# Layer 0 mixer of a two-layer diffusion backbone: projection and attention issued among the S5 batches, rotation tables on VectorE, attention normalised at its outputs

## The chip, the cores and the metric

One core of one Trainium2 chip runs the whole program. The metric is device time of one launch in microseconds (us). Engines: PE is TensorE, DVE is VectorE, ACT is ScalarE, POOL is GpSimd, SP issues the DMAs.

## The reference

Two layers are applied to 128 context tokens and 512 latent tokens (640 columns). The change touches the mixer of layer 0 only, which runs two head groups beside each other on one input projection:

```python
def _even_mixer_latent(h, ck, cv, x0_re, x0_im, w_in, w_out, s5p, rpb):
    u, q, k, v = _even_split(h, w_in)                 # u: 512 columns, q k v: 8 heads of 64
    a_out, _, _ = _s5_mixer(u, x0_re, x0_im, *s5p)
    b_out = _neighbourhood_attention(q, k, v, ck, cv, rpb)
    return concatenate([a_out, b_out], -1) @ w_out
# S5: x_t = lam_bar * x_(t-1) + b_bar u_t (complex, 32 groups, 64 states), forward and backward,
#     y = Re(c x) summed over both directions + d u; z = gelu(y); out = z * sigmoid(z @ w_glu + b_glu)
# attention: p = softmax([q k_window + bias, q ck]); out = p_loc v_window + p_ctx cv
```

The context tokens go through the same mixer with a zero start state and plain softmax attention. The rest (modulation, squared-ReLU MLP, the DeltaNet of layer 1, norms) is the same before and after.

## The kernel before

Every large matmul splits its f32 weights into a high and a low part (`weight`: ACT writes `whi`, L194; `wlo` is a subtraction, L196) and issues three matmuls per 128x128 weight tile (L205 to L207), 320 columns each. `self.lov = 3` around the projection puts two of three `wlo` subtractions on DVE, the others on POOL.

**S5.** The 32 groups go through in four batches of 8 (`s5_batch`), each with two directions d (`s5_unit`). A unit builds input taps `bp` (L785 to L787) and output taps `ct` (L798 to L800) on DVE, transposes `bp` (L792), computes `W` from the inputs `U` (L809), and turns the complex recurrence into a real one: `rotate` multiplies by a table `rt` of cosines and sines (L832, L833, after a swap of the halves by two DMAs, L825 and L826) and adds (L834), one real scan runs (L844 or L846), and a second `rotate` turns back. For d = 0 the adds L787 and L834 run on POOL, for d = 1 on DVE. `s5_taps` makes the taps inside a chunk (L914, L919), `s5_back` the outputs (L947 to L951) and the GELU (L964 to L969).

The table of a batch comes from `s5_tables`: a copy of nine start values (L877), then three doublings from 8 to 64 entries in `turns` (L863 to L868, six POOL operations each), then three DMAs that copy it to the other partitions and to the second direction (L880, L881). `rt` has two buffers, which are the two directions of one batch: the next table starts when the last rotations of the batch before are done with them.

**Attention.** For four head pairs five blocks of 128 queries: scores (L1003) into tags `pa` and `pc`, bias (L1008), maximum (L1010), its negation (L1011), exponential with sum on ACT (L1013), reciprocal (L1015), normalisation of the probabilities on POOL (L1017); three blocks later the transposes (L1023), the products with v (L1031) and the split into high and low part (L1040, L1041). `att` lies where the normed input `hn` of the projection was, so it opens when the projection is done.

**Order.** The program is written down once; a scheduler with a cost model of its own places every instruction on its engine's queue, by data and by priority. Before, the four batches stand first (priority 4000), the projection follows at lower priority and fills in, attention stands after both. Each queue then runs strictly in order.

Of the kernel before, what the change touches and what calls it, by code (L numbers as in the profile page):

```python
# [148 lines left out]
class Build:  # L149
# [465 lines left out]
    def s5_params(self, P, sm, ring):  # L615
# [151 lines left out]
        self.turns(e[:, 0], e[:, 1], 1, 8, wk[:, 2], wk[:, 3], nc.gpsimd)  # L767

    def s5_unit(self, b, d, P, U, tb):
# [17 lines left out]
        (V if d else nc.gpsimd).tensor_tensor(bpv, bpv, t1[:, :, :8], op=AD)  # L787
# [66 lines left out]
    def turns(self, c, s, n0, n1, w1, w2, eng):  # L854

        M, AD, SU = ALU.mult, ALU.add, ALU.subtract
        n = n0
        while n < n1:
            xr, xi = c[:, :, 1:n + 1], s[:, :, 1:n + 1]
            yr = c[:, :, n:n + 1].to_broadcast(list(xr.shape))  # L860
            yi = s[:, :, n:n + 1].to_broadcast(list(xr.shape))
            a1, a2 = w1[:, :, :n], w2[:, :, :n]
            eng.tensor_tensor(a1, xr, yr, op=M)  # L863
            eng.tensor_tensor(a2, xi, yi, op=M)
            eng.tensor_tensor(c[:, :, n + 1:2 * n + 1], a1, a2, op=SU)
            eng.tensor_tensor(a1, xr, yi, op=M)
            eng.tensor_tensor(a2, xi, yr, op=M)
            eng.tensor_tensor(s[:, :, n + 1:2 * n + 1], a1, a2, op=AD)  # L868
            n *= 2

    def s5_tables(self, b, P):

        nc = self.nc
        t = [self.tl([128, 2, 8, 65], "rt") for d in range(2)]
        w1 = self.PA.tile([128, 8, 32], F32, name="rt1")
        w2 = self.PA.tile([128, 8, 32], F32, name="rt2")
        nc.gpsimd.tensor_copy(t[0][:, :, :, 0:9], self.s5e[:, :, 8 * b:8 * b + 8])  # L877
        self.turns(t[0][:, 0], t[0][:, 1], 8, 64, w1, w2, nc.gpsimd)
# [14 lines left out]

    def s5_batch(self, b, P, U):
        ct, S = [None] * 2, [None] * 2
        tb = self.s5_tables(b, P)
        for d in range(2):
            ct[d], S[d] = self.s5_unit(b, d, P, U, tb[d])
        return U, ct, S
# [75 lines left out]
    def attention(self, hp, qkv, ab, P):  # L975
# [16 lines left out]
        def block(qs, keys, vts, kind):  # L992

            n = len(vts) * 128
            sc = []
# [9 lines left out]
            if kind is None:  # L1005
                V.tensor_copy(S[:, :, :n], two(pl, n))
            else:
                V.tensor_tensor(S[:, :, :256], two(pl, 256), biases[kind], op=ALU.add)  # L1008
                nc.scalar.activation(S[:, :, 256:n], two(pc, 128), AF.Copy)
            V.tensor_reduce(ss[:, :, 0:1], S[:, :, :n], axis=AX.X, op=ALU.max)  # L1010
            V.tensor_scalar(ss[:, :, 1:2], ss[:, :, 0:1], -1.0, None, op0=ALU.mult)  # L1011
            for hh in range(2):
                nc.scalar.activation(S[:, hh, :n], S[:, hh, :n], AF.Exp, bias=ss[:, hh, 1:2],  # L1013
                                     accum_out=ss[:, hh, 2:3])
            V.reciprocal(ss[:, :, 3:4], ss[:, :, 2:3])  # L1015
            for hh in range(2):
# [12 lines left out]
            for hh in range(2):  # L1029
                for i, v in enumerate(vts):  # L1030
                    nc.tensor.matmul(po[64 * hh:64 * hh + 64, 0:128], v[:, 64 * hh:64 * hh + 64],  # L1031
                                     pT[hh][:, 128 * i:128 * i + 128], start=(i == 0), stop=(i == len(vts) - 1),
                                     tile_position=(0, 64 * hh))
            if kind is None:
                o, hi, lo = po[:, 0:128], *(t[:, 0:128] for t in ab)
            else:
                o = po[:, 0:128].rearrange("p (c r) -> p c r", r=8)
                c0 = (qs.start - 128) // 8
                hi, lo = (t[:, 128:].rearrange("p (r c) -> p c r", r=8)[:, c0:c0 + 16] for t in ab)
# [31 lines left out]
    def even_s5(self, hn, P, fillers):  # L1071
# [13 lines left out]
        def ev(n, h, p):  # L1085
# [32 lines left out]
        def project():  # L1118
            def fill(m):
                for f in fillers[2 * m:2 * m + 2]:  # L1120
                    self.mod_half(*f, P, tag="pa")
            self.lov = 3
            self.gemm([A["wine"][4 + n] for n in range(12)], hn, ev, after=fill)
            self.lov = 0
        ust = self.ust
        zs = []
        held = None
        Us = [self.s5_load(t) for t in ust[:2]]
        for b in range(5):
            if b and b + 2 - 1 < 4:  # L1130
                Us.append(self.s5_load(ust[b + 2 - 1]))
            with tc.high_priority(offset=4000):
                cur = self.s5_batch(b, P, Us[b]) if b < 4 else None
                if cur:
                    kd = self.s5_taps(b, P, cur[1])
            if held:
                with tc.high_priority(offset=-1000):
                    zs.append(self.s5_back(b - 1, P, *held))
            held = (*cur, self.s5_pull(kd)) if cur else None
# [3 lines left out]
        fo = P.tile([64, 128], F32, name="fo")  # L1143
        V.tensor_copy(fo, fp[:64, :128])
        nc.sync.dma_start(out=self.O["sr"].rearrange("a b d g n -> (a b d g) n"), in_=fo[:, 0:64])
        nc.sync.dma_start(out=self.O["si"].rearrange("a b d g n -> (a b d g) n"), in_=fo[:, 64:128])
        with tc.high_priority(offset=-500):
            project()
        return zs, qkv
# [701 lines left out]
    def run(self, stop=None):  # L1851
        nc, A, tc = self.nc, self.A, self.tc
        with contextlib.ExitStack() as es:
# [35 lines left out]
            with contextlib.ExitStack() as ph:  # L1889
# [11 lines left out]
                with phase("l0") as P:  # L1901
# [5 lines left out]
                    zds, qkv = self.even_s5(hn, P, mods[:0])  # L1907
                    mods = mods[0:]
                    rx.close()
                    with phase("att", "right") as PA:  # L1910
# [17 lines left out]
                    with tc.high_priority(offset=1000):  # L1928
                        ads = self.even_gate(zds, P)
# [66 lines left out]
```

## Time and profile before

| | us |
|---|---|
| median of 3 runs (range) | 2006.68 (2005.63 to 2009.8) |
| profiled execution | 2007.75 |
| its span, first to last instruction | 2005.9 |
| mixer of layer 0, from the last S5 parameters to the gate's end | about 80 to 388 |

PE is busy 90% of the span, DVE 64%, ACT 43%, POOL 45%. The profiled execution lies 1.07 us above the median and 1.85 us above its own span. A busy PE is not PE at its peak: matmuls overlap, and its granted clock varies. The stretch in question is therefore read by itself, with its own waits.

### The profile page before, as it was taken

What the parts mean: (1) busy time and instruction counts of PE and PEld (TensorE: products, weight loads), DVE (VectorE), ACT (ScalarE), POOL (GpSimd) and SP (SyncE); (2) the same over time, 40 slices, a digit from 0 to 9 for tenths busy, and PEclk for the clock granted to TensorE, in tenths of its full rate; (3) what the DMA queues carried; (4) which work ended last, traced back from release to release, by engine and by line L of the source; (5) the groups of instructions that cost most, each with busy time, mean ns of one, the idle gap of its engine ahead of it and who ended that gap; (6) DMA issues with size and microseconds to landing.
All of it is one profiled execution on the core that took longest, in us unless ns stands there. A gap on an engine that the chain in (4) does not pass through costs nothing. (4 is left out here: it accounts for less than half of the span.)

```text
span 2005.9 us, 35754 instructions
## 1 busy us (share of the span) xinstructions
PE 1808.1 (90%) x13476; PEld 1705.7 (85%) x13476; DVE 1285.6 (64%) x2765; ACT 864.1 (43%) x1908; POOL 894.7 (45%) x743
## 2 busy tenths in 40 slices
PE   5778769998999999999888789888998899999998
PEld 3778757897899999998878788787888899999998
DVE  8877866638546372727779998865657936354453
ACT  4333345434326161626554365444324534444362
POOL 2766545362334343454466645532235234334351
PEclk9889889998999999999989899898989899999999
DMA  8334588623422222332586468758844122222221
GB/s 314 111 108 131 133 246 287 237 85 137 158 95 95 73 89 70 113 125 80 154 230 185 124 172 221 210 160 282 284 158 148 63 85 76 83 74 85 84 88 61
DMA packets 206984, 286.60 MB, mean 143 GB/s; under 512 B 54878, under 2 KB 138236, under 8 KB 206812
## 3 DMA queue, kind: packets, MB, share of 16 engines
q1 hardware_dynamic: 206812, 284.33, 44.5%
q8 instruction: 106, 1.74, 0.4%
q14 instruction: 66, 0.54, 0.1%
HBM read 228.87 MB, written 46.82 MB: 137 GB/s over the span
## 5 line engine op out<-in xcount | busy, mean ns | idle before, releaser
L196 POOL TENSOR_TENSOR wlo<-raw,whi 128x1024 fp32r<-128x1024 f32 (+1 forms) x145 | 335.1, 2313 | 393.9 <-ACT whi L194 378.9
L194 ACT ACTIVATE whi<-raw 128x1024 fp32r<-128x1024 f32 (+1 forms) x153 | 153.0, 1000 | 321.1 <-PE pg L206 144.1
L207 PE MATMUL pg<-hidh,wlo 128*128 128x320 f32 (+2 forms) x576 | 178.8, 311 | 0.6 <-POOL wlo L196 0.6
L205 PE MATMUL pg<-hidh,whi 128*128 128x320 f32 (+2 forms) x576 | 179.1, 311 | 0.0
L206 PE MATMUL pg<-hidl,whi 128*128 128x320 f32 (+2 forms) x576 | 179.0, 311 | 0.0
L205 PE MATMUL pg<-h10h,whi 128*128 128x320 f32 x472 | 158.5, 336 | 17.4 <-ACT cb L1312 11.1
L422 DVE SCALAR_TENSOR_TENSOR x<-pg,mod,x 128x128 f32<-128x128 f32 (+2 forms) x132 | 53.8, 436 | 179.5 <-PE pg L207 179.4
L206 PE MATMUL pg<-h10l,whi 128*128 128x320 f32 x472 | 156.4, 331 | 0.0
L207 PE MATMUL pg<-h10h,wlo 128*128 128x320 f32 x472 | 156.1, 331 | 0.0
L205 PE MATMUL pa<-hidh,whi 128*128 128x320 f32 x448 | 138.0, 310 | 2.8 <-ACT whi L194 2.8
L207 PE MATMUL pa<-hidh,wlo 128*128 128x320 f32 x448 | 138.4, 309 | 0.0
L206 PE MATMUL pa<-hidl,whi 128*128 128x320 f32 x448 | 138.2, 309 | 0.0
L422 DVE SCALAR_TENSOR_TENSOR x<-pa,mod,x 128x128 f32<-128x128 f32 (+2 forms) x108 | 43.9, 435 | 137.2 <-PE pa L207 137.2
L507 POOL TENSOR_TENSOR wq<-S,wq 128x512 fp32r<-128x512 f32 x52 | 70.7, 1360 | 115.6 <-ACT wq L506 115.6
L205 PEld LDWEIGHTS pg<-h10h,whi 128*128 128x128 f32 x472 | 95.8, 203 | 19.9 <-ACT cb L1312 11.6
L207 PEld LDWEIGHTS pg<-hidh,wlo 128*128 128x128 f32 x576 | 108.2, 188 | 1.6 <-POOL wlo L196 1.1
L205 PEld LDWEIGHTS pg<-hidh,whi 128*128 128x128 f32 x576 | 108.3, 188 | 0.9 <-issue 0.8
L206 PEld LDWEIGHTS pg<-hidl,whi 128*128 128x128 f32 x576 | 108.2, 188 | 0.4 <-DVE hidl L568 0.3
L1320 DVE SCALAR_TENSOR_TENSOR cv<-cb,cw,cv 128x642 f32<-128x642 f32 x90 | 94.5, 1051 | 7.8 <-ACT cv L1317 6.9
L206 PEld LDWEIGHTS pg<-h10l,whi 128*128 128x128 f32 x472 | 96.3, 204 | 0.6 <-issue 0.4
L207 PEld LDWEIGHTS pg<-h10h,wlo 128*128 128x128 f32 x472 | 95.9, 203 | 0.4
L205 PEld LDWEIGHTS pa<-hidh,whi 128*128 128x128 f32 x448 | 83.9, 188 | 4.4 <-ACT whi L194 3.6
(751 smaller groups left out, 5912.5 us busy)
## 6 DMA issues: line engine op xcount, KB each, us to landing
raw<-in_wff SPq DMA_DIRECT2D x104, 512.0 KB
mraw<-in_wmod SPq DMA_DIRECT2D x96, 512.0 KB
raw<-in_wino SPq DMA_DIRECT2D x33, 512.0 KB
rawx<-in_wff SPq DMA_DIRECT2D x24, 512.0 KB
raw<-in_wine SPq DMA_DIRECT2D x16, 512.0 KB
cka<-pd SPq DMA_DIRECT2D x28, 256.0 KB
ckb<-pd SPq DMA_DIRECT2D x28, 256.0 KB
s5g<-s5g SPq DMA_DIRECT2D x32, 164.0 KB
```

The costliest lines, as they stand in the source:

```text
L194: nc.scalar.activation(hi[:, :kt], raw[:, :kt], AF.Copy)
L196: (nc.vector if self.lov and self.nw % self.lov else nc.gpsimd).tensor_tensor(lo[:, :kt], raw[:, :kt], hi[:, :kt], op=ALU.subtract)
L205: nc.tensor.matmul(p[:, :n], hi[:, k], xh[:, s], start=(k == 0), stop=False)
L206: nc.tensor.matmul(p[:, :n], hi[:, k], xl[:, s], start=False, stop=False)
L207: nc.tensor.matmul(p[:, :n], lo[:, k], xh[:, s], start=False, stop=(k == kt - 1))
L422: nc.vector.scalar_tensor_tensor(x[m][:, s], p[:, ls], g, x[m][:, s], op0=ALU.mult, op1=ALU.add)
L507: (V if j % 2 else nc.gpsimd).tensor_tensor(t[:, 4:8], src, t[:, 0:4], op=SU)
L1320: V.scalar_tensor_tensor(cv, cb[m][:, t:t + 642], cw[:, t:t + 1], cv, op0=M, op1=AD)
```

## The change

Four parts. (1) `turns` works on cosine and sine together: four DVE operations per doubling in place of six on POOL. (2) The adds L787 and L834 of d = 0 go to DVE like those of d = 1. (3) `even_s5` no longer raises and lowers priorities: a generator `s5_steps` yields after each table and each direction. Three steps (batch 0) stand ahead of the projection, one step after every second of its 12 weight tiles (batches 1 and 2), and one after each attention block (batch 3, the last outputs). `self.lov = 3` is gone, so all 12 `wlo` of the projection are on POOL. (4) Attention keeps its exponentials unnormalised; the reciprocal sums are spread over partitions by two matmuls a block against the identity, copied by ACT, and multiplied onto the outputs by DVE. The maximum comes out negated from the reduction, the context block reads its scores in PSUM, and `pT` gets tiles of its own. The copies `ko` and `fo` for the outputs share the three buffers `s5o` of `s5_back`.

```diff
-        self.turns(e[:, 0], e[:, 1], 1, 8, wk[:, 2], wk[:, 3], nc.gpsimd)
+        self.turns(e, 1, 8, wk.rearrange("p a b c -> p (a b c)"))
...
-        (V if d else nc.gpsimd).tensor_tensor(bpv, bpv, t1[:, :, :8], op=AD)
+        V.tensor_tensor(bpv, bpv, t1[:, :, :8], op=AD)
...
-            (V if d else nc.gpsimd).tensor_tensor(out, m, sw, op=op)
+            V.tensor_tensor(out, m, sw, op=op)
...
-            eng.tensor_tensor(a1, xr, yr, op=M)
-            eng.tensor_tensor(a2, xi, yi, op=M)
-            eng.tensor_tensor(c[:, :, n + 1:2 * n + 1], a1, a2, op=SU)
-            eng.tensor_tensor(a1, xr, yi, op=M)
-            eng.tensor_tensor(a2, xi, yr, op=M)
-            eng.tensor_tensor(s[:, :, n + 1:2 * n + 1], a1, a2, op=AD)
+            V.tensor_tensor(a, x, yi, op=M)
+            V.tensor_tensor(y, x, yr, op=M)
+            V.tensor_tensor(y[:, 0], y[:, 0], a[:, 1], op=SU)
+            V.tensor_tensor(y[:, 1], y[:, 1], a[:, 0], op=AD)
...
-                V.tensor_copy(S[:, :, :n], two(pl, n))
+                src = two(pl, n)
...
-            V.tensor_reduce(ss[:, :, 0:1], S[:, :, :n], axis=AX.X, op=ALU.max)
-            V.tensor_scalar(ss[:, :, 1:2], ss[:, :, 0:1], -1.0, None, op0=ALU.mult)
+            V.tensor_reduce(ss[:, :, 1:2], src, axis=AX.X, op=ALU.max, negate=True)
...
-                nc.gpsimd.tensor_scalar(S[:, hh, :n], S[:, hh, :n], ss[:, hh, 3:4], None, op0=ALU.mult)
...
-            pT = [self.tl([128, 384], tag) for tag in ("bp", "bpt")]
+            pT = [P.tile([128, 384], F32, name=f"pT{hh}") for hh in range(2)]
...
+                nc.tensor.matmul(po[64 * hh:64 * hh + 64, 128:256], ss[:, hh, 3:4].to_broadcast([128, 64]), self.ident,
+                                 start=True, stop=True, tile_position=(0, 64 * hh))
+            nc.scalar.activation(rs, po[:, 128:256], AF.Copy)
+            V.tensor_tensor(po[:, 256:384], po[:, 0:128], rs, op=ALU.mult)
...
-                ko = self.tl([128, 128], "ko")
+                ko = self.tl([128, 656], "s5o")[:, 0:128]
...
+        steps = self.s5_steps(P)
+        for _ in range(3):
+            next(steps)
+        def after(m):
+            if m % 2:
+                next(steps)
+        self.gemm([A["wine"][4 + n] for n in range(12)], hn, ev, after=after)
...
                                 open_.append(blk)
+                                next(steps, None)
```

On POOL, at the first table of the S5 batches, before (L877 starts a table, L863 to L868 double it, L787 is the add of `bp`):

```order
L877 COPY rt<-s5e 128x16x9
L940 MEMSET s5o 128x8
L863 TENSOR_TENSOR rt_1080<-rt 128x8x8
L864 TENSOR_TENSOR rt_1081<-rt 128x8x8
L865 TENSOR_TENSOR rt<-rt_1080,rt_1081 128x8x8
L866 TENSOR_TENSOR rt_1080<-rt 128x8x8
L867 TENSOR_TENSOR rt_1081<-rt 128x8x8
L868 TENSOR_TENSOR rt<-rt_1080,rt_1081 128x8x8
L787 TENSOR_TENSOR bp<-bp,s5tmp 128x1024
```

The same place on POOL now (L875 is the copy that starts a table, L196 the low part of a weight):

```order
L1054 MEMSET us 128x8x18 x2
L875 COPY rt<-s5e 128x16x9
L196 TENSOR_TENSOR wlo<-raw,whi 128x1024 x3
L931 MEMSET s5o 128x8
L196 TENSOR_TENSOR wlo<-raw,whi 128x1024
L875 COPY rt<-s5e 128x16x9
L196 TENSOR_TENSOR wlo<-raw,whi 128x1024 x3
```

Between two table starts only weight splits are left. On DVE, where attention begins, before (L832 to L844 are the rotation and scan of batch 3, L1006 the first score copy):

```order
L832 TENSOR_TENSOR s5g<-s5g,rt 128x8x65
L832 TENSOR_TENSOR s5g<-s5g,rt 128x8x17
L833 SCALAR_TENSOR_TENSOR s5g<-s5g,cst,rt 128x8x65
L833 SCALAR_TENSOR_TENSOR s5g<-s5g,cst,rt 128x8x17
L839 MEMSET s5g 128x8
L840 MEMSET s5g 128x8
L844 SCALAR_TENSOR_TENSOR s5g<-s5g 128x656
L1006 COPY sS<-pa 128x2x128
```

On DVE at the same point now (L834 to L867 belong to batch 2 and to the table of batch 3, L1001 is the first maximum):

```order
L834 TENSOR_TENSOR s5s<-s5g 128x656
L864 TENSOR_TENSOR rt_2595<-rt 128x128
L865 TENSOR_TENSOR rt<-rt 128x16x8
L787 TENSOR_TENSOR bp<-bp,s5tmp 128x1024
L851 COPY s5fin<-s5s 128x8
L814 COPY s5g<-s5prm 128x8
L866 TENSOR_TENSOR rt<-rt,rt_2595 128x8x8
L867 TENSOR_TENSOR rt<-rt,rt_2595 128x8x8
L1001 TENSOR_REDUCE ss<-pa 128x2
L799 TENSOR_TENSOR s5tmp<-pwi,s5bc_757 128x1152
```

Attention starts one batch earlier, with the whole of batch 3 still to come on DVE. On PE at the same point, before (L792 and L809 serve batch 3, L1003 are scores):

```order
L792 MATMUL pb<-cst,bp 128x128 x8
L207 MATMUL pg<-h00h_126,wlo 128x320
L1110 MATMUL pc<-cst,qs 128x128
L809 MATMUL pb<-s5s,bpt 128x128 x7
L809 MATMUL pb<-s5s,bpt 128x82
L1110 MATMUL pc<-cst,qs 128x128 x7
L1003 MATMUL pa<-kT,qz_2893 128x128
```

On PE now (L792 and L809 serve batch 2, L993 are scores, L905 the taps of batch 2, L1011 a transpose of probabilities):

```order
L1105 MATMUL pc<-cst,qs 128x128
L792 MATMUL pb<-cst,bp 128x128 x8
L1105 MATMUL pc<-cst,qs 128x128 x7
L809 MATMUL pb<-s5s,bpt 128x128 x7
L809 MATMUL pb<-s5s,bpt 128x82
L993 MATMUL pa<-kT,qz_2569 128x128
L281 MATMUL pa<-mraw,scond 32x256 x4
L993 MATMUL pc<-ckT,qz_2569 128x128 x2
L993 MATMUL pa<-kT,qz_2570 128x128
L993 MATMUL pc<-ckT,qz_2570 128x128 x2
L905 MATMUL pb<-ct,Bb_923 32x128 x16
L1011 MATMUL pg<-cst,sS 128x128
```

The eight transposes and eight input products of a unit stand in both rows; before they are those of the last batch, now those of the last but one.

## Rows read from the trace of the kernel before

**Rows 1.** Stretches: length, then busy us (instructions) of PE, PEld, DVE, ACT, POOL; clock.
```profile
80.50:251.00 170.50, 138.51 (x972) 134.95 (x972) 131.37 (x160) 53.52 (x105) 114.28 (x101) 0.87 0.45 124
251.00:268.75 17.75, 3.18 (x27) 2.71 (x26) 5.16 (x9) 3.19 (x6) 6.46 (x7) 0.71 0.69 183
268.75:376.00 107.25, 105.60 (x873) 81.71 (x873) 77.67 (x198) 62.48 (x181) 55.15 (x51) 0.98 0.83 266
376.00:388.00 12.00, 9.41 (x54) 7.97 (x54) 9.03 (x12) 6.25 (x14) 4.78 (x2) 1.00 0.41 136
```
**Rows 2.** Waits from 80 to 270 us: who waited for whom, total, times, longest.
```profile
ACT s5g L811 <- POOL s5g L834: 32.7, 3, 11.3
DVE s5g L832 <- DMA rt<-rt: 27.8, 4, 11.3
...
PE pb L914 <- ACT s5g L811: 19.9, 3, 7.0
```
**Rows 3.** Timeline of DVE: the first rotation of each batch (start, us, idle before).
```profile
121.43 0.91 DVE L832 TENSOR_TENSOR s5g<-s5g,rt 128x520 f32<-128x520 f32 x2 [11.35 <-DMA rt<-rt]
...
166.73 0.70 DVE L832 TENSOR_TENSOR s5g<-s5g,rt 128x520 f32<-128x520 f32 x1 [6.48 <-DMA rt<-rt]
...
206.36 0.91 DVE L832 TENSOR_TENSOR s5g<-s5g,rt 128x520 f32<-128x520 f32 x2 [0.37 <-DMA rt<-rt]
...
262.52 0.91 DVE L832 TENSOR_TENSOR s5g<-s5g,rt 128x520 f32<-128x520 f32 x2 [9.64 <-DMA rt<-rt]
```
**Rows 4.** DVE from one first rotation to the next, and from the last to 388.
```profile
121.43:166.73 45.30, 37.55 (x46) 0.81 0.37 101
166.73:206.36 39.63, 33.53 (x44) 0.91 0.56 159
206.36:262.52 56.16, 39.05 (x49) 0.84 0.49 135
...
262.52:388.00 125.48, 90.01 (x216) 0.96 0.78 249
```
**Rows 5.** Timeline of POOL: start of two tables, and the end of the second.
```profile
85.42 1.37 POOL L877 COPY rt<-s5e 128x144 f32<-128x144 f32 x1
...
179.53 0.32 POOL L877 COPY rt<-s5e 128x144 f32<-128x144 f32 x1 [5.91 <-issue]
...
197.20 1.73 POOL L868 TENSOR_TENSOR rt<-rt,rt 128x256 f32<-128x256 f32 x1
```
**Rows 6.** Timeline of SP: the first table's DMAs are issued.
```profile
112.00 1.19 SPq L880 DMA_DIRECT2D rt<-rt  x2
```
**Rows 7.** Timeline of DVE: two products of f32 tiles with a broadcast operand.
```profile
80.51 0.29 DVE L743 TENSOR_TENSOR pw<-pwr 128x128 f32<-128x128 f32 x1
...
123.26 1.22 DVE L786 TENSOR_TENSOR s5tmp<-pwi,Bb 128x1024 f32<-128x1024 f32 x1
```
**Rows 8.** DVE groups, shapes apart, 82 to 388 us: count, busy, mean ns.
```profile
L196 DVE TENSOR_TENSOR wlo<-raw,whi 128x1024 fp32r<-128x1024 f32 x7 | 9.5, 1355 | 0.2 <-ACT whi L194 0.2
...
L787 DVE TENSOR_TENSOR bp<-bp,s5tmp 128x1024 f32<-128x1024 f32 x4 | 7.2, 1810 | 0.8 <-DVE s5tmp L786 0.8
...
L1041 DVE TENSOR_TENSOR ab<-pc,ab 128x128 fp32r<-128x128 f32 x20 | 7.2, 362 | 3.6 <-ACT ab L1040 3.3
...
L834 DVE TENSOR_TENSOR s5s<-s5g 128x656 f32<-128x656 f32 x4 | 4.6, 1146 | 0.0
...
L1011 DVE TENSOR_SCALAR ss<-ss 128x2 f32<-128x2 f32 x20 | 3.8, 197 | 0.0
```
**Rows 9.** PE group of attention's products with v, 269 to 376 us.
```profile
L1031 PE MATMUL pc<-bp,vt 128*64 128x128 f32 x72 | 12.1, 287 | 0.0
```
**Rows 10.** Timeline of PE: W of one unit; first and last product of one `s5_back`.
```profile
102.81 1.91 PE L809 MATMUL pb<-s5s,bpt 128*128 128x128 f32 x16
...
276.74 0.49 PE L947 MATMUL pb<-s5s,ct 128*128 128x128 f32 x2
...
283.09 0.39 PE L951 MATMUL pb<-s5s,L 128*128 128x81 f32 x2
```

More of the change, by code (lines that the diff above doesn't have):

```diff
@@ L852, in s5_unit, with turns @@
         return ct, S
-    def turns(self, c, s, n0, n1, w1, w2, eng):
+    def turns(self, t, n0, n1, w):
+        V = self.nc.vector
         M, AD, SU = ALU.mult, ALU.add, ALU.subtract
-        n = n0
+        n, g = n0, t.shape[2]
         while n < n1:
[L859 to L862, printed above, removed]
-            eng.tensor_tensor(a1, xr, yr, op=M)
-            eng.tensor_tensor(a2, xi, yi, op=M)
-            eng.tensor_tensor(c[:, :, n + 1:2 * n + 1], a1, a2, op=SU)
-            eng.tensor_tensor(a1, xr, yi, op=M)
-            eng.tensor_tensor(a2, xi, yr, op=M)
-            eng.tensor_tensor(s[:, :, n + 1:2 * n + 1], a1, a2, op=AD)
+            x, y = t[:, :, :, 1:n + 1], t[:, :, :, n + 1:2 * n + 1]
+            sh = [128, 2, g, n]
+            yr, yi = (t[:, k, :, n:n + 1].unsqueeze(1).to_broadcast(sh) for k in range(2))
+            a = w[:, :2 * g * n].rearrange("p (k g e) -> p k g e", k=2, g=g)
+            V.tensor_tensor(a, x, yi, op=M)
+            V.tensor_tensor(y, x, yr, op=M)
+            V.tensor_tensor(y[:, 0], y[:, 0], a[:, 1], op=SU)
+            V.tensor_tensor(y[:, 1], y[:, 1], a[:, 0], op=AD)
             n *= 2
@@ L892, in s5_load @@
         return U
[L894 to L899, printed above, removed]
     def s5_taps(self, b, P, ct):
@@ L1009, in block @@
                 nc.scalar.activation(S[:, :, 256:n], two(pc, 128), AF.Copy)
[L1010 to L1011 removed]
+                src = S[:, :, :n]
+            V.tensor_reduce(ss[:, :, 1:2], src, axis=AX.X, op=ALU.max, negate=True)
             for hh in range(2):
[L1013 removed]
+                nc.scalar.activation(S[:, hh, :n], src[:, hh], AF.Exp, bias=ss[:, hh, 1:2],
                                      accum_out=ss[:, hh, 2:3])
             V.reciprocal(ss[:, :, 3:4], ss[:, :, 2:3])
[L1016 to L1017 removed]
             yield
[L1019 removed]
+            pT = [P.tile([128, 384], F32, name=f"pT{hh}") for hh in range(2)]
             for hh in range(2):
@@ L1033, in block @@
                                      tile_position=(0, 64 * hh))
+            for hh in range(2):
+                nc.tensor.matmul(po[64 * hh:64 * hh + 64, 128:256], ss[:, hh, 3:4].to_broadcast([128, 64]), self.ident,
+                                 start=True, stop=True, tile_position=(0, 64 * hh))
+            rs = P.tile([128, 128], F32, name="rs")
+            nc.scalar.activation(rs, po[:, 128:256], AF.Copy)
+            V.tensor_tensor(po[:, 256:384], po[:, 0:128], rs, op=ALU.mult)
             if kind is None:
-                o, hi, lo = po[:, 0:128], *(t[:, 0:128] for t in ab)
+                o, hi, lo = po[:, 256:384], *(t[:, 0:128] for t in ab)
             else:
-                o = po[:, 0:128].rearrange("p (c r) -> p c r", r=8)
+                o = po[:, 256:384].rearrange("p (c r) -> p c r", r=8)
                 c0 = (qs.start - 128) // 8
@@ L1117, in ev @@
                 nc.sync.dma_start(out=qkv[hp][m], in_=tmp[n])
[L1118 to L1124, printed above, removed]
+        steps = self.s5_steps(P)
[4 more added lines that the diff above has]
+                next(steps)
@@ L1125, in even_s5, with s5_steps @@
+        self.gemm([A["wine"][4 + n] for n in range(12)], hn, ev, after=after)
+        return steps, qkv
+    def s5_steps(self, P):
+        nc = self.nc
+        self.zs = zs = []
         ust = self.ust
-        zs = []
         held = None
         Us = [self.s5_load(t) for t in ust[:2]]
[L1129 to L1135, printed above, removed]
-            if held:
-                with tc.high_priority(offset=-1000):
-                    zs.append(self.s5_back(b - 1, P, *held))
-            held = (*cur, self.s5_pull(kd)) if cur else None
+        for b in range(4):
+            if 1 <= b < 3:
+                Us.append(self.s5_load(ust[b + 1]))
+            ct, S = [None] * 2, [None] * 2
+            tb = self.s5_tables(b, P)
+            yield
+            ct[0], S[0] = self.s5_unit(b, 0, P, Us[b], tb[0])
+            yield
+            ct[1], S[1] = self.s5_unit(b, 1, P, Us[b], tb[1])
+            kd = self.s5_taps(b, P, ct)
+            if held:
+                zs.append(self.s5_back(b - 1, P, *held))
+            held = Us[b], ct, S, self.s5_pull(kd)
+            yield
+        zs.append(self.s5_back(3, P, *held))
+        yield
@@ L1141, in even_s5 @@
         fp = self.ps("pb")
         nc.tensor.transpose(fp[:64, :128], self.s5fin, self.ident)
-        fo = P.tile([64, 128], F32, name="fo")
-        V.tensor_copy(fo, fp[:64, :128])
+        fo = self.tl([128, 656], "s5o")[0:64, 0:128]
+        nc.vector.tensor_copy(fo, fp[:64, :128])
         nc.sync.dma_start(out=self.O["sr"].rearrange("a b d g n -> (a b d g) n"), in_=fo[:, 0:64])
         nc.sync.dma_start(out=self.O["si"].rearrange("a b d g n -> (a b d g) n"), in_=fo[:, 64:128])
-        with tc.high_priority(offset=-500):
-            project()
```

14 lines of the change are left out of this document (5 added, 9 removed).

## The prediction

> **What bounds the kernel now.** I read the stretches first, then the waits, then each queue's order of time in the stretch that the change touches. From 80.5 to 251 us the projection and S5 run together: PE is busy 138.5 of 170.5 us at a granted clock of 0.87, DVE 131.4, POOL 114.3; then PE has 3.2 us of work in 17.75 us until attention starts; from 268.75 to 376 PE is busy 105.6 of 107.25 us while DVE has 77.7 [rows 1]. So the first stretch is not PE's, the attention stretch is. The reader is to see in the waits who ends what in the first one: DVE waits 27.8 us in all for the table `rt`, ACT 32.7 us for POOL's rotation adds, PE 19.9 us behind that ACT copy [rows 2]. That is one chain: table on POOL, DMA, rotation, add on POOL, buffer free, W copied, PE goes on.
>
> The beat is the batch. First rotations start at 121.4, 166.7, 206.4 and 262.5 us [rows 3], 47.0 us apart on average, with 36.7 us of DVE work in each (37.55, 33.53, 39.05) [rows 4]. A table takes POOL from 179.53 to 198.93, 19.4 us [rows 5] with one rotation add inside, and its copies land later: the first is issued at 112.0 and waited for until 121.4, 9.4 us [rows 3, 6]. After the last first rotation 125.5 us remain to the gate's end at 388, with 90.0 us of DVE work [rows 4].
>
> **The change part by part.**
>
> *Tables on DVE.* Four operations in place of six per doubling, over 16n, 16n, 8n and 8n elements, n = 8, 16, 32: 2688 elements in 12 instructions. No row shows this operation on DVE. The nearest are 0.29 us for 128 elements and 1.22 for 1024 [rows 7]: 0.93/896 = 1.04 ns an element and 0.16 fixed. That gives 2.8 + 1.9 = 4.7 us a table. Bounds: 2.8 (elements alone) and 19.4 (POOL's own time); I take 4.7, as the rows are the same engine and type. The first table starts with POOL's at 85.4 [rows 5], but DVE's order puts both directions' `bp` and `ct` between its pieces; nine more products of 1.2 to 1.6 us and two adds give about 20.5 us, so its DMAs go out at 106 in place of 112.0 [rows 6]. With the same 9.4 us the first rotation comes at 115.5, 6 us earlier.
>
> *Adds on DVE.* Per batch one L787 at 1.8 us and two L834 at 1.0 (the row has 1.146) [rows 8]: 3.8 us. *Weight splits.* Seven of 1.36 us leave DVE in the stretch [rows 8], 2.3 us a batch; POOL has room for all twelve at about 2.4 us, since four tables were most of its 114 us [rows 1, 5]. *Work per batch on DVE:* 36.7 + 4.7 + 3.8 - 2.3 = 42.9 us, 6.2 more than before. Against that stands the idle time: of 47.0 us 10.3 were idle, and the waits for `rt` alone were 6.48, 0.37 and 9.64 [rows 3], 5.5 on average. After its last piece the table now has about 7 us of other DVE work in front of the rotation, which covers most of the 9.4. POOL's adds no longer stand inside the chain. I leave 4 us of waits and take 3 off for DVE operations that POOL slowed; a batch then takes 44 us (40 to 47). So the tables alone buy little per batch: DVE gives up a wait and gets the work instead.
>
> *Batch 3 behind the start of attention.* This is the main term. By the order rows attention's first maximum stands after the first rotations of batch 2, not of batch 3. First rotation of batch 2: 115.5 + 2 x 44 = 203.5. Attention starts 6.2 us after that rotation, as before (268.75 - 262.52) [rows 1, 3]: 210, in place of 268.75. PE can be there: of its 138.5 us, batch 3's unit, one `s5_back` and one set of taps leave (12), so 80.5 + 126.5 = 207. The vacated memory of `hn` and the loads of k and q, which PE waits for, move with it. SP's queue holds the swaps, the tables' copies, `s5_back`'s and the q, k, v loads in program order; a load behind a waiting swap is late, and that is in the 4 us.
>
> *What attention then carries.* On DVE: the 90.0 us of before, plus one whole batch 42.9, two more rotation adds 2.0, 20 products with the spread sums at the price of the nearest PSUM product, 0.362 [rows 8], 7.2; minus 20 negations of 0.197 [rows 8], 3.9, and four score copies of 256 elements, 1.7 estimated from 0.362 for half as many. Sum 136.5; less 3 for POOL's absence 133.5. On PE: unit (two times 1.9 for W [rows 10], the transposes at most as much), one back 276.74 to 283.48 less 1.5 of other work, 5.2 [rows 10], taps 1.1: about 12.5. The 40 spreading matmuls: 80 records at 12.1/72 = 0.168 us [rows 9] would be 13.4; half, if the two halves overlap in their column groups as those of L1031 do: 7. So PE needs 107.25 + 19.5 and the 12 us tail [rows 1], 139 us from 210, to 349. DVE needs 133.5 us of work from 203.5: to 337 without any wait, but both queues run in order and feed each other. Before, DVE idled 28% there because PE was the bound; in the S5 beat without the `rt` waits 12%. I take 14%, near the latter since DVE is now as full: 156 us, so the gate ends at 359.5 in place of 388.
>
> *Normalisation at the outputs.* POOL's multiplications, between exponential and transposes, go; POOL is idle half of that stretch [rows 1], so alone they hold nobody up. What is late next is the output: spread, ACT copy, DVE product, then the two split operations, while the PSUM slot `pc` stays held and PE's next context scores want it. ACT gets 20 copies, some 7 us beside 62.5 of 107 [rows 1]: no bound. `ko` in `s5o` buffers makes an ACT copy wait for `s5_back`'s buffers; at most a few us on an engine with slack, 0 taken.
>
> *Sum.* 359.5 - 388 = -28.5. From 388 to the end the same instructions run, in queues that the scheduler shuffled a little: 0, within 6. From the profiled execution's 2007.75 this gives 1979; the median of the runs lies 1.07 lower, so the sum stands for 1978 to 1979. I predict 1980.
>
> A page's rule would move the beat. The first table took POOL 26.6 us, from 85.4 to 112.0, the third 19.4, each with one add inside [rows 5, 6]: the same operations last differently beside a busy DVE. The Trainium skill, "SBUF — State Buffer", section "SBUF: two separate sides", says that a GpSimd operation and a VectorE operation with two SBUF inputs hold their shared ports exclusively, so that the later one blocks. By it DVE would run at its shortest durations once the tables are gone, about 40 us a batch, which is the quick case below; but the twelve weight splits, now all on POOL, would block DVE in turn, which is why I don't take it whole. The trace of before agrees as far as those two table times go.
>
> **The rivals.**
>
> *Quick case: PE stays attention's bound.* Batches take 40 us (first rotation of batch 2 at 195.5, attention at 202), DVE's work hides beside PE, and the gate ends 139 + 8 us later, at 349. 39 us less: 1969. For it: PE was busy 105.6 of 107.25 us there [rows 1]. Against: DVE's 133.5 us are within 4% of PE's sum.
>
> *Slower: DVE becomes the bound of attention and PE waits in it.* The batch's rotations, scans and taps stand on one queue between the scores' bias and maximum; a wait for a swap then delays the softmax of three open blocks, PE waits for the transposes, and `pc` is held longer. If DVE keeps the 28% idle that it has there now [rows 4], 133.5 us become 186: from 203.5 to 389.5, 2009; with batches of 47 us from 209.5 to 395.5, 2015. It decides from 51 us of waits on. For it: 42.9 + 7.2 us more work on an engine that already took turns with PE. Against: its waits there were PE's, and with less work. The Trainium skill, "Perfetto Trace Analysis", section "Optimizing Scalar/DVE Operations", advises moving work off a saturated VectorE, to GpSimd even, and this change goes the other way; the trace of before has DVE at 77% in S5 and 72% in attention, not yet saturated.
>
> *The change doesn't move attention forward.* The loads of q and k stand behind waiting swaps on SP, and the projection behind waiting S5 matmuls on PE; attention starts only at 235 and carries the batch all the same: 235 + 151 = 386, 2006. Against: PE's 126.5 us of work end well ahead.
>
> **How the numbers follow.** Forecast, 1970 to 1994: 0.56. Quick case, 1945 to 1970: 0.17. No earlier start or gains given back, 1995 to 2010: 0.15. Slower by DVE as the bound, 2011 and more: 0.12. A measurement of this kernel can tell 0.2%, 4 us, from no change. Faster than 2002.7: 0.56 + 0.17 + 0.06 = 0.79; within 4 us either way: 0.09; slower: 0.12. The range leaves out 0.1 at each end: 1955 to 2012 holds the bounds of batch (40 to 47, 8 us each way), of waits in attention (147 to 168 in place of 156) and part of the slower case; the forecast's own is 1970 to 1994.
>
> **What would show it.** Right: first rotations at about 115, 160 and 204, `rt` no longer among DVE's long waits, the first scores near 210, DVE over 80% busy from there to the gate's end near 360, POOL below 35 us in the S5 stretch. Wrong: batches 47 us or more apart with DVE waiting for swaps; scores after 225; PE idle over 25 us in attention with DVE or `pc` as the releaser; or a difference after 388 above 6 us.

## The result, and the profile after

The changed kernel takes 1976.73 us (median of 4 runs, 1975.02 to 1986.26), the kernel before beside it 2006.16 (1999.24 to 2009.80): ratio 0.9874, interval 0.9854 to 0.9894. That is 29 us less; the prediction said 1980. The profiled execution took 1976.35 us with a span of 1974.1. Run once more, in a later group of runs, it came out at the same ratio (0.9876, below).

First the stretches of the changed kernel: S5 with the projection, the gap until the first scores, attention, and the gate (columns as in [rows 1]).

```profile
80.50:205.00 124.50, 108.73 (x800) 105.60 (x799) 112.79 (x174) 44.80 (x85) 35.02 (x19) 0.96 0.57 151
205.00:215.79 10.79, 4.30 (x36) 3.68 (x34) 6.63 (x13) 5.32 (x12) 1.19 (x2) 0.90 0.60 162
215.79:349.00 133.21, 121.28 (x1071) 96.21 (x1072) 103.58 (x247) 71.95 (x213) 7.95 (x11) 0.97 0.76 239
349.00:361.00 12.00, 9.62 (x65) 8.46 (x65) 8.78 (x12) 5.71 (x13) 4.76 (x2) 0.97 0.39 138
```

Against [rows 1] the S5 stretch is 46 us shorter (124.5 for 170.5), at a granted clock of 0.96 for 0.87, and POOL has 35 us in it for 114. Attention is 26 us longer (133.2 for 107.25), as it now carries the last S5 batch. The waits of DVE and PE from 80 to 270 us (columns as in [rows 2]):

```profile
DVE s5g L833 <- DMA s5g<-s5g: 9.6, 6, 2.7
DVE s5g L832 <- DMA rt<-rt: 6.9, 4, 3.0
...
PE pb L792 <- DVE bp L787: 9.8, 2, 5.3
PE pa L993 <- DMA qz<-qkv: 5.4, 1, 5.4
...
PE pg L207 <- POOL wlo L196: 2.2, 2, 1.9
```

The wait for the table fell from 27.8 to 6.9 us, and PE's 19.9 us behind the ACT copy of `s5g` are gone. Of POOL's work only the weight splits still keep PE waiting, twice and 2.2 us in all. The timeline, in order: DVE's four first rotations, PE's first scores, DVE's last gate operation and first residual.

```profile
117.23 0.70 DVE L832 TENSOR_TENSOR s5g<-s5g,rt 128x520 f32<-128x520 f32 x1 [0.52 <-DMA rt<-rt]
...
157.76 0.70 DVE L832 TENSOR_TENSOR s5g<-s5g,rt 128x520 f32<-128x520 f32 x1 [1.76 <-DMA rt<-rt]
...
203.14 0.91 DVE L832 TENSOR_TENSOR s5g<-s5g,rt 128x520 f32<-128x520 f32 x2 [3.04 <-DMA rt<-rt]
...
215.79 0.77 PE L993 MATMUL pa<-kT,qz 128*128 128x128 f32 x2 [5.45 <-DMA qz<-qkv]
...
254.47 0.70 DVE L832 TENSOR_TENSOR s5g<-s5g,rt 128x520 f32<-128x520 f32 x1 [1.56 <-DMA rt<-rt]
...
359.16 0.69 DVE L1185 SCALAR_TENSOR_TENSOR s5tmp<-s5s,L 128x256 fp32r<-128x256 f32 x1 [0.22 <-ACT L L1184]
363.65 0.68 DVE L422 SCALAR_TENSOR_TENSOR x<-pg,mod,x 128x128 f32<-128x128 f32 x2 [3.80 <-PE pg L207]
```

The kernel before had its first residual and its first store of `xd`, the end of layer 0, here (the store's row gives min/median/max ns, then first and last start):

```profile
390.44 0.68 DVE L422 SCALAR_TENSOR_TENSOR x<-pg,mod,x 128x128 f32<-128x128 f32 x2 [3.29 <-PE pg L207]
...
L1963 SPq DMA_DIRECT2D xd<-x x8: 326/326/327, 861.8 to 914.3; - x8
```

The scores start 53 us earlier and the first residual comes 26.8 us earlier. By the first store of `xd` the difference is 29.2 us (832.6 for 861.8), and at the span's end 31.8. The batches did not become quicker for it: the first two gaps between first rotations are 40.5 and 45.4 us, 43.0 on average, and the same two gaps were 45.3 and 39.6 before, 42.5 on average. The 47.0 us of before are the mean of three gaps, and the third, 56.2 us, lies where the projection ends and DVE waits 9.64 us for the table [rows 3, 4]. Batch 2's first rotation comes only 3.2 us earlier than before. What moved is attention: it now starts behind that rotation and not behind the next one. DVE between first rotations, and from the third one to 360 (columns as in [rows 4]):

```profile
117.23:157.76 40.53, 36.81 (x60) 0.96 0.54 146
157.76:203.14 45.38, 39.38 (x59) 1.00 0.67 185
203.14:254.47 51.33, 41.88 (x87) 0.93 0.81 231
203.14:360.00 156.86, 119.91 (x272) 0.97 0.73 225
```

The operations that the change puts in, as groups of DVE and PE (count, busy us, mean ns of one, idle before):

```profile
L787 DVE TENSOR_TENSOR bp<-bp,s5tmp 128x1024 f32<-128x1024 f32 x8 | 11.8, 1472 | 0.1
L834 DVE TENSOR_TENSOR s5s<-s5g 128x656 f32<-128x656 f32 x8 | 6.8, 847 | 0.1
...
L1028 DVE TENSOR_TENSOR pc<-pc,rs 128x128 f32<-128x128 f32 x20 | 5.8, 290 | 1.5 <-ACT rs L1027 1.5
L865 DVE TENSOR_TENSOR rt<-rt 128x512 f32<-128x512 f32 x4 | 2.7, 679 | 0.0
L864 DVE TENSOR_TENSOR rt<-rt 128x512 f32<-128x512 f32 x4 | 2.7, 678 | 0.0
...
L1024 PE MATMUL pc<-cst,ss 128*64 128x128 f32 x80 | 12.4, 279 | 0.0
```

The group means of the twelve doubling operations (L864 to L867, three sizes each) add up to 4.54 us a table, forecast 4.7.

### The profile page after: what moved, and what is told of

It reads as the page before. It is cut to its first block, busy times and chain, and to the rows that moved or that the text cites. A ratio compares the mean times of both kernels' runs of the same rounds, so it can differ in the third digit from the quotient of the medians.

```text
span 1974.1 us, 35755 instructions
## 1 busy us (share of the span) xinstructions
PE 1799.6 (91%) x13556; PEld 1698.3 (86%) x13556; DVE 1290.8 (65%) x2825; ACT 869.5 (44%) x1928; POOL 760.8 (39%) x609
## 5 line engine op out<-in xcount | busy, mean ns | idle before, releaser
L196 POOL TENSOR_TENSOR wlo<-raw,whi 128x1024 fp32r<-128x1024 f32 (+1 forms) x153 | 360.8, 2361 | 512.6 <-ACT whi L194 466.6
```

The lines of the kernel that those rows point to most:

```text
L196: (nc.vector if self.lov and self.nw % self.lov else nc.gpsimd).tensor_tensor(lo[:, :kt], raw[:, :kt], hi[:, :kt], op=ALU.subtract)
```

## The experiments

The kernels keep the whole computation. "Residual" is the start of the first residual of layer 0 in the profiled run, which is where the mixer ends; the ratio is to runs of the kernel before on the same chip (medians 2007.1 to 2007.4 for the experiments).

| kernel | projection's last matmul | first scores | residual | median us | ratio (95%) |
|---|---|---|---|---|---|
| before | 250.9 | 268.75 | 390.44 | 2006.16 | |
| changed | 205.1 | 215.79 | 363.65 | 1976.73 | 0.9874 (0.9854 to 0.9894) |
| changed, again | 204.7 | 214.94 | 361.24 | 1981.51 | 0.9876 (0.9859 to 0.9894) |
| 1 parts 1, 2 alone | 204.6 | 215.81 | 366.37 | 1974.03 | 0.9831 (0.9814 to 0.9847) |
| 2 order alone | 222.6 | 229.60 | 377.40 | 1991.79 | 0.9928 (0.9911 to 0.9946) |
| 3 old attention | 204.7 | 214.89 | 362.20 | 1969.27 | 0.9806 (0.9791 to 0.9821) |
| 4 batch 3 early | 206.0 | 216.24 | 364.33 | 1978.33 | 0.9856 (0.9840 to 0.9873) |
| 5 attention held | 205.4 | 261.87 | 383.94 | 1994.58 | 0.9931 (0.9913 to 0.9948) |
| 6 part 1 alone | 226.3 | 239.47 | 372.40 | 1982.89 | 0.9873 (0.9855 to 0.9891) |
| 7 part 2 alone | 242.3 | 252.80 | 375.69 | 1996.13 | 0.9940 (0.9919 to 0.9961) |
| 8 splits on DVE | 244.6 | 267.25 | 395.98 | 2001.31 | 0.9968 (0.9949 to 0.9986) |
| 9 part 4 alone | 250.4 | 267.96 | 391.01 | 2003.89 | 0.9987 (0.9969 to 1.0005) |
| 10 `ct` on POOL | 227.4 | 231.29 | 376.75 | 2000.13 | 0.9966 (0.9947 to 0.9984) |
| 3 again | 205.0 | 214.32 | 362.74 | 1969.37 | 0.9815 (0.9785 to 0.9845) |

**1, parts 1 and 2 alone.** The kernel before with

```diff
-        self.turns(t[0][:, 0], t[0][:, 1], 8, 64, w1, w2, nc.gpsimd)
+        self.turns(t[0], 8, 64, w)
-        (V if d else nc.gpsimd).tensor_tensor(bpv, bpv, t1[:, :, :8], op=AD)
+        V.tensor_tensor(bpv, bpv, t1[:, :, :8], op=AD)
-            (V if d else nc.gpsimd).tensor_tensor(out, m, sw, op=op)
+            V.tensor_tensor(out, m, sw, op=op)
```

> The kernel before with parts 1 and 2 alone: rotation tables doubled on VectorE and the running-sum adds on VectorE; the old order of layer 0 (projection tiles, four batches, attention), the old normalisation, the splits on VectorE as they were. My theory (the gain is that attention starts one batch earlier; the tables only let the batches follow faster): first rotations near 116, 160, 204 and 248 us, first scores near 254, end of the mixer's gate 373 to 376 (before: 387), so 10 to 15 us under the kernel before, ratio 0.993 to 0.995, less than half of what the whole change gives. Rival 'it is the tables alone' (GpSimd's chain was the bound and the order is idle): 25 to 30 us under, ratio 0.986. Rival 'it is the normalisation': 0, ratio 1.000.

Measured 0.9831: my theory's 10 to 15 us were missed, the rival's 25 to 30 exceeded (33 us, of which 24.1 lie in the mixer). The early start that I ascribed to the order is there without it. The row is PE's first score in this kernel:

```profile
215.81 0.43 PE L1001 MATMUL pa<-kT,qz 128*128 128x128 f32 x2
```

The four batches still stand first in the code, at the higher priority. The scheduler nevertheless ended the projection at 204.6 us and let attention start behind it. DVE between the first rotations of batches 0, 1 and 2 (all columns as in [rows 1]):

```profile
119.97:159.11 39.14, 35.53 (x263) 34.54 (x262) 31.78 (x59) 14.66 (x29) 3.07 (x2) 0.91 0.51 137
159.11:192.70 33.59, 31.43 (x258) 30.50 (x257) 29.81 (x56) 15.00 (x29) 3.03 (x2) 1.00 0.58 161
```

DVE has the tables and the adds on top of its old work and is yet busy for less of a gap, 31.8 and 29.8 us for 37.6 and 33.5 before [rows 4]: with POOL nearly idle (3 us a gap) its own operations are shorter. The scan L844 took 2.60 us on average in the kernel before and takes 1.52 here; the last section shows how.

**2, order alone.** `s5_steps` among the projection and attention, GpSimd's tables and adds kept.

```diff
-            with tc.high_priority(offset=4000):
-                cur = self.s5_batch(b, P, Us[b]) if b < 4 else None
+        steps = self.s5_steps(P)
...
+        self.gemm([A["wine"][4 + n] for n in range(12)], hn, ev, after=after)
```

> The kernel before with the new order alone: projection and attention among the batches, tables and running-sum adds still on GpSimd, old normalisation. My theory: tables still take some 19 us on GpSimd, batches 45 to 47 us apart, first rotation of batch 2 near 215, first scores near 222 (before: 268.75), the gate's end near 370, so 15 to 20 us under the kernel before, ratio 0.990 to 0.992. Rival 'it is the tables alone': 0 to 3 us, ratio 0.999 to 1.000; it would also hold if the new order only moves GpSimd's wait for the tables into attention. Rival 'it is the normalisation': 0, ratio 1.000.

Near my theory: batches 47.0 us apart (122.36, 171.19, 216.45), 15 us gained, 13.0 of them in the mixer. The ratio, 0.9928, and the scores, 229.6 for 222, lie just outside what it said.

**3, the old attention block** in the changed kernel, run twice:

```diff
+                nc.gpsimd.tensor_scalar(S[:, hh, :n], S[:, hh, :n], ss[:, hh, 3:4], None, op0=ALU.mult)
...
-            V.tensor_tensor(po[:, 256:384], po[:, 0:128], rs, op=ALU.mult)
```

> The changed kernel with the old attention block: scores negated and multiplied by the reciprocal on GpSimd ahead of the transposes, no spreading matmuls, no product behind the output matmul. My theory: the normalisation at the outputs holds nobody up, and neither did the old one: within 4 us of the changed kernel on either side, ratio to the kernel before 0.985 to 0.990. Rival 'it is the normalisation' (GpSimd's multiplies sat on the chain from scores to outputs): 10 us or more over the changed kernel, ratio 0.992 or more.

> The changed kernel itself, on one chip with the others of this group. If normalising at the outputs costs time, as the run with the old attention block suggests (1969 us), the changed kernel comes out 5 to 9 us over that, 1974 to 1979, ratio to the kernel before 0.985 to 0.989. If that difference was only one between chips, it comes out at 1967 to 1972, ratio 0.980 to 0.983.

> The changed kernel with the old attention block once more, on one chip with the others of this group. If it is faster than the changed kernel by its program (another order of layer 1's instructions), the ratio to the kernel before comes out at 0.979 to 0.983 again; if the first result was the chip's, 0.985 to 0.989 as the changed kernel had twice.

The mixer ends within 2 us of the changed kernel, as forecast. The whole was not as forecast: it is 7 to 12 us quicker than the changed kernel (medians 1969.3 and 1969.4 against 1976.7 and 1981.5), and the intervals of the ratio don't overlap in either run. Where, the first store of `xd` shows (min/median/max ns, then first and last start); in the old attention block's kernel, span 1966.8, it is

```profile
L1961 SPq DMA_DIRECT2D xd<-x x8: 326/326/327, 832.9 to 885.4; - x8
```

and in the changed kernel, span 1974.1,

```profile
L1965 SPq DMA_DIRECT2D xd<-x x8: 326/326/327, 832.6 to 885.1; - x8
```

So layer 0 ends at the same time in both, and the difference is all in layer 1, whose code neither edit touches but whose instructions the scheduler places anew: of the 1626 operations that DVE has behind this point in either kernel, 800 stand at the same place of its queue. The changed kernel itself, profiled again, stored `xd` at 831.6 and ended at 1984.8: with the same order layer 1 differs by 11.7 us between two executions of one program. That the order makes the medians differ is therefore likely, and not shown by a run of its own.

**4, batch 3 early.** The changed kernel with four steps taken behind the projection:

```diff
         self.gemm([A["wine"][4 + n] for n in range(12)], hn, ev, after=after)
+        for _ in range(4):
+            next(steps)
```

> The changed kernel with the last of the four S5 batches put back ahead of attention (its four steps are taken right behind the projection). My theory: first scores one batch later, near 255 us (215.8 in the changed kernel); VectorE's work of that batch no longer lies under attention and attention's no longer beside it, so 12 to 18 us over the changed kernel, ratio to the kernel before 0.993 to 0.997. Rival 'it is the tables alone' or 'it is the normalisation': as the changed kernel, ratio 0.986 to 0.989.

Nothing moved: first scores at 216.24 us, ratio as the changed kernel. The place in the code does not hold attention back: the scores still come 39 us ahead of batch 3's first rotation (255.20), as the scheduler fills in by data. So this run could not test what early attention is worth, and the next one holds it by data.

**5, attention held.** As 4, and

```diff
+            V.tensor_copy(self.hold, Z[:, 0, 8:9])          # batch 3, d = 0, after its first rotation
...
+        V.tensor_copy(kT[:, 0:1], self.hold)
         nc.sync.dma_start(out=kT, in_=qkv[0])
```

> The changed kernel with attention held back by data: its first loads of k wait for a value of batch 3's first rotation (one copied element; nothing computed changes). Theory A (the tables matter because the projection ends sooner and attention starts a batch sooner): first scores near 262 us, then attention's 107 us and the tail of 12, gate's end near 381, so 17 to 24 us over the changed kernel, ratio to the kernel before 0.995 to 0.999. Theory B (the early start is a by-product; the gain is VectorE's and GpSimd's shorter chain, and attention without a batch beside it runs that much quicker): within 8 us of the changed kernel, ratio at most 0.991.

Theory A for the mixer: first scores at 261.87, the first residual 20.3 us later than in the changed kernel. The gate ends 18 us later (378.1 for 359.9), the first store of `xd` comes 15 us later (848.0 for 832.6), and 13 us are left in the whole (median 1994.58 against 1981.51 on the same chip), less than A's 17 to 24 and more than B's 8. The two stretches, from 80.5 to the scores and on to the residual:

```profile
80.50:261.87 181.37, 137.80 (x1048) 131.45 (x1046) 155.13 (x261) 60.04 (x116) 37.14 (x21) 0.91 0.59 161
261.87:383.94 122.07, 114.68 (x952) 90.68 (x951) 79.80 (x187) 68.59 (x205) 12.50 (x11) 0.97 0.65 215
```

Attention by itself takes 122.1 us to the residual, as before (268.75 to 390.44: 121.7), for 147.9 with the batch beside it. To the first residual, the changed kernel starts attention 46 us earlier and pays 26 for the batch beside it: 20 are left.

**6 and 7, parts 1 and 2 apart.** The first edit of 1 alone, and the other two alone.

> The kernel before with part 1 alone: the doublings of the table on VectorE; running-sum adds still on GpSimd. Theory A1 (GpSimd's 19 us tables hold up rotation, PE's queue and so the projection): most of the gain of parts 1 and 2 together, first scores at 215 to 222 us, 25 to 33 us under the kernel before, ratio 0.983 to 0.988. Theory A2 (it was the adds in the chain): 0 to 10 us under, ratio 0.995 or more.

> The kernel before with part 2 alone: the running-sum adds on VectorE; the doublings of the table still on GpSimd. Theory A1 (it is the tables): 0 to 8 us under the kernel before, first scores not before 255 us, ratio 0.996 to 1.000. Theory A2 (the adds, which stood behind tables on GpSimd's queue and in front of PE's): 15 us or more under, ratio 0.992 or less.

Each theory had a share. The tables alone give 24 us (A1's 25 to 33 just missed, its scores at 215 to 222 clearly: 239.5), the adds alone 11 (between what A1 and A2 had). With the adds gone and the tables still on POOL, first rotations come at 120.24, 165.09, 206.57 and 248.35, 42.7 apart; attention then starts 16 us earlier and the mixer ends 14.7 earlier. Each edit takes one of POOL's two kinds of work out of the chain. In the mixer the tables give 18.0 us, the adds 14.8 and both together 24.1, so the two overlap; in the whole it is 24, 11 and 33.

**8, splits on DVE** in the kernel before (`self.lov = 3` becomes 100).

> The kernel before with all weight splits of the projection on VectorE (self.lov = 100): no low part of a weight stands behind a table on GpSimd any more. Theory A (GpSimd's tables and adds hold up the rotations, and by them PSUM and PE's queue; the splits are no part of it): the projection's last matmul stays at 240 us or later (before: 250.9), ratio to the kernel before 0.998 to 1.005. Theory B (the tables delay the splits and so the projection): last matmul by 230 us, ratio 0.993 or less.

Theory B falls: the projection still ends at 244.6, and the mixer is 5.5 us later. Theory A's ratio of at least 0.998 was missed too (0.9968), but what was gained comes behind layer 0: the first store of `xd` is 2.6 us later than before (864.4).

**9, part 4 alone** in the kernel before (`pT` in its old slots).

> The kernel before with part 4 alone: attention normalised at its outputs (pT in its old slots). From the run with the old attention block, where the mixer ended within 2 us of the changed kernel and the rest of the difference came after layer 0: the mixer's end within 4 us of the kernel before (first residual at 386 to 394 us, before: 390.4), whole ratio 0.996 to 1.004, which is the spread that other orders of layer 1 gave. Rival 'normalisation at the outputs is a gain of its own': first residual by 382, ratio 0.994 or less. Rival 'it costs': first residual after 396, ratio over 1.004.

Nothing: 0.6 us in the mixer, and an interval that holds 1 for the whole.

**10, `ct` on POOL,** in the kernel of 3:

```diff
-        V.tensor_tensor(t2, bc4(self.pi[:, ps], 3, sh), bc4(self.C2[:, ps], 2, sh), op=M)
-        V.tensor_tensor(ct, ct, t2, op=SU)
+        G.tensor_tensor(t2, bc4(self.pi[:, ps], 3, sh), bc4(self.C2[:, ps], 2, sh), op=M)
+        G.tensor_tensor(ct, ct, t2, op=SU)
```

> The changed kernel with the old attention block, and the second product and the subtraction of the output taps (L799, L800) on GpSimd, which is idle in the S5 stretch. If VectorE's work per batch is what is left as the beat (40 to 45 us a batch, VectorE over 90% busy there), 5.5 us less per batch on it end the projection 5 to 10 us sooner (204.7 in the kernel without this edit) and the mixer 3 to 10 us sooner; ratio to the kernel before 0.976 to 0.980. If PE is the bound by now, or GpSimd's slower operations come into the chain: the mixer's end as without the edit or later, ratio 0.980 to 0.985.

The forecast failed: 31 us lost, 14 of them in the mixer, batches 49.2 and 48.2 us apart (117.64, 166.84, 215.04). POOL's groups in this kernel, one group of DVE's, and the S5 stretch up to the projection's end (columns as in [rows 1]):

```profile
L800 POOL TENSOR_TENSOR ct<-ct,s5tmp 128x1152 f32<-128x1152 f32 x8 | 24.6, 3081 | 4.9 <-DVE ct L798 4.6
L799 POOL TENSOR_TENSOR s5tmp<-pwi,s5bc 128x1152 f32<-128x1152 f32 x8 | 19.2, 2403 | 43.6 <-DVE bp L787 32.4 <-DVE ss L1002 6.9 <-DVE s5g L815 4.3
...
L865 DVE TENSOR_TENSOR rt<-rt 128x512 f32<-128x512 f32 x4 | 7.1, 1782 | 0.0
...
80.50:227.50 147.00, 117.20 (x807) 113.76 (x806) 125.10 (x174) 46.44 (x89) 70.03 (x31) 0.88 0.50 137
```

DVE did the two in 1.62 and 1.60 us in the changed kernel. POOL takes 2.4 and 3.1 and sits idle 43.6 us in front of the first, in a queue that waits for DVE and is waited for by it. The load did not fall either. DVE lost two operations a unit and is busy 125.1 us of 147.0 up to the projection's end, where the kernel of 3 has 112.7 of 124.5: what it kept takes longer beside POOL, such as a doubling of the table, L865 at 1.78 us for 0.68. Of the 22 us that the stretch is longer, 12 are busy time of DVE and 10 its waits.

The Trainium skill, "Perfetto Trace Analysis", section "Optimizing Scalar/DVE Operations", says that offloading some work from a saturated VectorE, even to GpSimd, may make sense, and adds that between these two it might not help, as they share a read port of SBUF. The prediction named only the first half. The second is what runs 1, 6, 7 and 10 show: work that left POOL for DVE made the mixer 15 to 24 us shorter, and work that left DVE for POOL made it 14 longer.

The quickest version is that of 3, 38 us below the kernel before. The changed kernel with `self.lov = 3` back around the projection was not tried.

## Why the prediction was right, and where it was not

*Tables on DVE:* 4.7 us each and first rotation at 115.5; measured 4.54 and 117.23. *Work and beat of a batch:* 42.9 us, less 3 for contention, in 44; measured 38.1 in 43.0 (mean of two). The adds cost 3.15 us a batch (1.472 + 0.847 + 0.832) where 3.8 were taken; waits were 4.9 for 4. *First rotation of batch 2:* 203.5; measured 203.14. The 44 us came true as a length, but not as 3 us less than 47: over these two gaps the kernel before had 42.5. The beat that the tables and adds alone give is 36.4 us (run 1); with the order and the splits of the change it is 43.0.

*Attention's start:* 210, measured 215.8. The step took the distance of the kernel before, 6.2 us behind a rotation. But the start hangs on the projection: in all the runs but the held one it follows the projection's last matmul by 4 to 23 us, 10.7 in the changed kernel, for q and k on their way through memory. PE was there at 205 where 207 was forecast; the way from there was not in the sum.

*From batch 2's first rotation to the gate's end:* 156 us, measured 156.9, but by two errors that cancel. DVE has 119.9 us of work, not 133.5, and 24% idle, not 14%. The products cost 0.290 us each, not 0.362. The rest of the 13.6 us is in the main the size of a batch. The prediction took 36.7 us from a trace in which POOL slowed DVE, and only 3 off for that; in run 1 a gap holds 30 to 32 us of DVE work with tables and adds in it, where the sum has 42.9 less 3. Single rows agree: L787 and L834 take 1.47 and 0.85 us for 1.81 and 1.15 [rows 8]. How the 13.6 us divide is not settled beyond that. DVE was therefore 76% busy, and the sign "over 80%" failed. PE was busy 130.9 us (121.3 and 9.6) where 139 were forecast, although the spreading matmuls cost 12.4 and not 7. The 139 are in part lengths of stretches; with PE's busy time in them [rows 1] the sum is 134.5.

*Normalisation:* 0 for the mixer; shown from both sides (3 and 9). *Weight splits:* no cost on the chain was forecast. Run 8 shows that only for the kernel before; in the changed one they lengthen DVE's operations, four products of the output taps alone by 8.6 us in all (last section), and no run shows what that costs the mixer.

*After 388:* 0 within 6. Measured -2.4 in layer 0's rest and -2.6 in layer 1, but +8.1 in all for the changed kernel's second profile, more than the 6 that the prediction called a sign of being wrong; layer 1's own 11.7 us between two executions cover it.

The step that failed is the attribution. The prediction called the new order the main term and had the tables "buy little per batch". The mechanism, attention starting a batch sooner, held: held back by data, the mixer loses 20 of its 27 us at the first residual (15 of 29 at the first store of `xd`). But the order isn't what starts it. Parts 1 and 2 alone moved the projection's end from 250.9 to 204.6, attention with it, and the mixer's end by 24.1 us; the order alone reaches 222.6 and 13.0 us; and on top of parts 1 and 2 the order, with the splits moved to POOL, gives 4 us of the mixer (366.4 to 362.2, runs 1 and 3). Both edits shorten the same thing, so their gains don't add: 24 and 13 us of the mixer alone, 28 together (run 3).

What I had overlooked is that the projection fills in: its place in the queues seems to follow from how long the scheduler expects the S5 chain to take. No line or priority of the projection differs between run 1 and the kernel before, and it ends 46 us sooner. PE's queue in the two traces says how much of that can be the plan. Before, the projection's last matmul stands behind the input products (L809) of seven of the eight S5 units; in runs 1 and 6 (tables moved) behind six, in run 7 (adds alone) behind seven, with the new order behind five. The sixth unit's products start at 194.2 us in run 1 and at 208.6 before, so 14 of the 46 us were won by the quicker chain ahead of them. The other 32 lie behind them: before, 105 of the projection's 672 matmuls were still to come there, 35 of them behind the seventh unit's products at 243.3; in run 1 only 51 were, and none behind a seventh. How those 32 us divide between the plan and the waits that went stays open.

The rivals: no earlier start is out (215.8 us). The slower case needed 51 us of DVE waits from batch 2's rotation on and got 37. The quick case's rotation at 195.5 came in run 1 (192.70), but the scores stayed at 215.8.

The 1980 us were therefore hit partly by luck: the two errors in DVE's work and idle time cancel, and the early start came from the parts that were thought to buy little.

## What to carry to other kernels

Look whose queue a dependent chain passes through, and which engines' operations lengthen each other, not only how busy the engines are: taking the slower engine out of the chain gave 24 us of the mixer here, putting it back into another place cost 14. An overlap gives the earlier start less what the overlapped work costs (46 less 26), so measure it by holding the consumer back by data; the place in the code may hold nothing. Where a scheduler places everything, compare the end of the changed part as well as the whole, since untouched code gets another order.

## What the runs showed of the hardware

The same DVE operation takes longer where POOL is busy beside it. The output taps in the kernel of run 1, with three weight splits on POOL from 82 to 300 us:

```profile
L799 DVE TENSOR_TENSOR s5tmp<-pwi,s5bc 128x1152 f32<-128x1152 f32 x8 | 10.8, 1355 | 0.0
L800 DVE TENSOR_TENSOR ct<-ct,s5tmp 128x1152 f32<-128x1152 f32 x8 | 10.8, 1347 | 0.0
L798 DVE TENSOR_TENSOR ct<-pwr,s5bc 128x1152 f32<-128x1152 f32 x8 | 10.5, 1346 | 0.0
```

and in the changed kernel, with ten of 2.9 us:

```profile
L798 DVE TENSOR_TENSOR ct<-pwr,s5bc 128x1152 f32<-128x1152 f32 x8 | 14.9, 1894 | 0.0
L799 DVE TENSOR_TENSOR s5tmp<-pwi,s5bc 128x1152 f32<-128x1152 f32 x8 | 13.0, 1622 | 0.1
L800 DVE TENSOR_TENSOR ct<-ct,s5tmp 128x1152 f32<-128x1152 f32 x8 | 12.8, 1603 | 0.0
```

That is 1.07 us a unit, 8.6 us over eight, and the timeline of the changed kernel shows where they lie:

```profile
109.52 1.34 DVE L799 TENSOR_TENSOR s5tmp<-pwi,s5bc 128x1152 f32<-128x1152 f32 x1
109.76 3.35 POOL L196 TENSOR_TENSOR wlo<-raw,whi 128x1024 fp32r<-128x1024 f32 x1 [14.70 <-ACT whi L194]
110.90 3.42 DVE L800 TENSOR_TENSOR ct<-ct,s5tmp 128x1152 f32<-128x1152 f32 x1
...
120.35 2.89 POOL L196 TENSOR_TENSOR wlo<-raw,whi 128x1024 fp32r<-128x1024 f32 x1 [7.20 <-ACT whi L194]
120.92 3.53 DVE L799 TENSOR_TENSOR s5tmp<-pwi,s5bc 128x1152 f32<-128x1152 f32 x1
...
125.81 1.33 DVE L800 TENSOR_TENSOR ct<-ct,s5tmp 128x1152 f32<-128x1152 f32 x1
```

Four of the 24 products took 3.42 to 3.55 us, the others 1.33 to 1.36. Each of the four starts while a split runs on POOL and ends 1.21 or 1.22 us after it, as if it had done next to nothing until then. It holds the other way round too: the split at 109.76 starts inside a DVE product and takes 3.35 us, where the shortest took 2.35. The Trainium skill, "SBUF — State Buffer", section "SBUF: two separate sides", says that such pairs lock each other out of their shared ports. These rows agree: a DVE product that came second took 2.1 to 2.2 us more. The two long scans of the kernel before (L844, 3.69 and 3.66 us for 1.52) also lie beside work of POOL.

PE's granted clock, a mean of its two levels (1.2 and 2.4 GHz) over a stretch, was 0.87 in the S5 stretch of the kernel before, with PE busy 138.5 of 170.5 us, 0.96 in that of the changed kernel, with 108.7 of 124.5, and 0.76 from 205 to 262 us of run 5, where attention was held back and PE had 30.6 us of work in 57. In the 10.8 us gap of the changed kernel, with 4.3 us of work, it was 0.90.
